# Splitting the 128-row transfers of a cross-entropy kernel into 32-row transfers

## The chip, the cores and the metric

The kernel runs on one core of a Trainium2 chip. The metric is the device time in microseconds of one execution; the times shown are medians of several executions.

## The reference

Two float32 matrices of 8192 x 8192 come in, and one goes out. Nothing is reduced: each output element depends on one element of each input.

```python
eps = 1e-7
pred = np.clip(pred, eps, 1 - eps)
return -(target * np.log(pred) + (1 - target) * np.log(1 - pred))
```

`target` holds zeros and ones only. The kernel uses that: for such a target the result is -log|target - 1 + pred|, so one logarithm is enough.

## The kernel before

The 67.1 million elements are taken as a flat list and cut into 37 chunks, numbered 0 to 36, from the end of the list to its beginning. A chunk is laid on all 128 partitions, so that partition p holds one contiguous piece of DRAM (`chunk`). Chunks 0 and 1 are 7680 columns wide, chunks 2 to 33 are 15360 wide (61440 bytes of float32 a row), chunks 34 and 35 are 7680 wide, and chunk 36 has 1696 columns. A further 45056 elements at the start of the list, "side", are held on 32 partitions and moved by SP in transfers of eight rows.

Two rings in on-chip memory hold the chunks: `ring_p`, float32, for `pred`, and `ring_t`, bfloat16, for `target`. The target is cast by the transfer itself. Each ring has two places of 15360 columns, which chunks take in turn, so chunk k + 2 goes where chunk k was. All arithmetic is done in place in `ring_p`, and the store reads from it. Therefore the load of pred of chunk k + 2 has to wait until the store of chunk k has read its last byte, whereas the load of its target needs only that DVE is done with the old one.

For each wide chunk the work is done in two halves of 7680 columns: DVE clips pred (L90) and adds target - 1 (L93), ACT takes the absolute value (L96) and the logarithm (L97), and DVE negates (L100). The order on each engine is written out by hand (`manual_schedule`). POOL issues almost all transfers, in this order for each chunk k: the store of chunk k (L76), the target load of chunk k + 2 (L71), the pred load of chunk k + 2 (L72). Its queue is in order: an instruction that waits holds those behind it. SP issues the first pred load, the side transfers and the last three stores. One transfer of 128 rows is spread over the core's 16 DMA engines, eight rows on each.

Chunk 33 is called z in the last part of the code, and chunks 34, 35 and 36 are a, b and c. The last loads are issued while chunk 32 is stored, and then the remaining stores drain.

Of the kernel before, what the change touches and what calls it, by code (L numbers as in the profile page):

```python
# [1 line left out]

# [4 lines left out]

EPS = 1e-7

BIG = 15 * 1024  # L10
HALF = BIG // 2
SIDE = 1408


def plan(total):

    n, last = divmod(total, BIG)
    assert n > 4 and 0 < last <= 2048
    spots = [(HALF, 0), (HALF, HALF)]
    spots += [(BIG, k % 2 * BIG) for k in range(1, n - 1)]  # L20
    end = (n - 1) % 2 * BIG
    return spots + [(HALF, end), (HALF, end + HALF), (last - SIDE // 4, 2 * BIG)]

@with_exitstack
def kernel(
    ctx: ExitStack,
    tc: tile.TileContext,
    pred: bass.AP,  # L30
    target: bass.AP,
    out: bass.AP,
):
    nc = tc.nc
    fp32 = mybir.dt.float32
    bf16 = mybir.dt.bfloat16
    Alu = mybir.AluOpType
    Act = mybir.ActivationFunctionType
    P = nc.NUM_PARTITIONS

    R, C = pred.shape
    spots = plan(R * C // P)
    n = len(spots)
    widths = [w for w, _ in spots]
    cols = [sum(widths[:k]) for k in range(n)]

    def chunk(ap, k):
        flat = ap.rearrange("r c -> (r c)")
        end = R * C - cols[k] * P
        return flat[end - widths[k] * P : end].rearrange("(p w) -> p w", p=P)  # L50

    pool = ctx.enter_context(tc.tile_pool(name="rings", bufs=1))
    ring = [P, 2 * BIG + widths[-1]]
    ring_p = pool.tile(ring, fp32, name="ring_p", tag="ring_p")
    ring_t = pool.tile(ring, bf16, name="ring_t", tag="ring_t")
    warm = pool.tile([1, 8], fp32, name="warm", tag="warm")
    side_p = pool.tile([32, SIDE], fp32, name="side_p", tag="side_p")
    side_t = pool.tile([32, SIDE], fp32, name="side_t", tag="side_t")

    def side(ap, j):  # L60
        flat = ap.rearrange("r c -> (r c)")
        return flat[: 32 * SIDE].rearrange("(p w) -> p w", p=32)[j:32:4]

    def spot(ring, k, part=(0, 1)):
        w, c = spots[k]
        i, m = part
        return ring[:, c + i * w // m : c + (i + 1) * w // m]

    def load(k):
        queue = nc.sync if k == 0 else nc.gpsimd  # L70
        nc.gpsimd.dma_start(out=spot(ring_t, k), in_=chunk(target, k))  # L71
        queue.dma_start(out=spot(ring_p, k), in_=chunk(pred, k))  # L72

    def store(k):
        queue = nc.sync if k >= n - 3 else nc.gpsimd
        queue.dma_start(out=chunk(out, k), in_=spot(ring_p, k))  # L76

    def load_side():
        nc.vector.memset(side_p[:, 0:2], 0.5)  # L79
        nc.vector.memset(side_t[:, 0:2], 0.0)  # L80
        for j in range(4):
            nc.sync.dma_start(out=side_t[j:32:4, :], in_=side(target, j))
            nc.sync.dma_start(out=side_p[j:32:4, :], in_=side(pred, j))

    def store_side():
        for j in range(4):
            nc.sync.dma_start(out=side(out, j), in_=side_p[j:32:4, :])

    def front_of(p, t):
        nc.vector.tensor_scalar(  # L90
            out=p, in0=p, scalar1=EPS, scalar2=1 - EPS, op0=Alu.max, op1=Alu.min
        )
        nc.vector.scalar_tensor_tensor(  # L93
            out=p, in0=t, scalar=1.0, in1=p, op0=Alu.subtract, op1=Alu.add
        )
        nc.scalar.activation(out=p, in_=p, func=Act.Abs)  # L96
        nc.scalar.activation(out=p, in_=p, func=Act.Ln)  # L97

    def back_of(p):
        nc.vector.tensor_scalar(out=p, in0=p, scalar1=-1.0, scalar2=None, op0=Alu.mult)  # L100

    def front(k, *part):
        front_of(spot(ring_p, k, *part), spot(ring_t, k, *part))

    def back(k, *part):
        back_of(spot(ring_p, k, *part))

    with tc.manual_schedule():
        nc.vector.memset(warm, 1.0)  # L109
        for k in range(3):  # L110
            load(k)
        nc.scalar.activation(out=warm, in_=warm, func=Act.Ln)  # L112
        front(0)
        front(1)
        back(0)
        store(0)
        back(1)
        store(1)
        load(3)
        for k in range(2, n - 4):  # L120
            front(k, (0, 2))
            front(k, (1, 2))
            back(k, (0, 2))
            back(k, (1, 2))
            store(k)
            if k == n - 6:
                load_side()
            if k == n - 5:
                front_of(side_p, side_t)
            for j in range(k + 2, n if k == n - 5 else k + 3):  # L130
                load(j)
        z, a, b, c = range(n - 4, n)
        front(z, (0, 2))
        back_of(side_p)
        store_side()
        front(z, (1, 2))
        back(z, (0, 2))
        front(a)
        back(z, (1, 2))
        store(z)  # L140
        front(b, (0, 2))
        front(b, (1, 2))
        back(a)
        store(a)
        front(c)
        back(b)
        store(b)
        back(c)
        store(c)


# [1 line left out]
_INS = ['pred', 'target']  # L153
_OUTS = [((8192, 8192), 'float32')]


# [23 lines left out]
```

## Time and profile before

| what | value |
|---|---|
| time, median of 3 executions | 1865.55 us (1865.36 to 1867.03) |
| profiled execution, span from its first to its last instruction | 1863.1 us |
| DVE, ACT, POOL busy in it | 1124.7, 902.1, 57.4 us |
| HBM read and written | 536.87 MB and 268.44 MB |
| transfers issued by POOL, by lines L71, L72, L76 | 37, 36, 34 |
| one POOL issue, mean | 0.53 to 0.54 us |

No time but its span is kept for the profiled execution; the median is 2.45 us above the span. The profile's page gives busy times of the engines, the share of time in which the 16 DMA engines moved packets, and the packets of each queue (q0 is POOL's, q1 is SP's). A packet here is one row of a transfer, or one small write that tells a semaphore of a completion. The trace holds a record of every packet with its size, start and duration, without the number of the DMA engine.

### The profile page before, as it was taken

Reading aid. Unit: us, or ns where it says so; the run is one execution under the profiler, and the core shown is the slowest. Engines: PE = TensorE matmul, PEld = TensorE weight load, DVE = VectorE, ACT = ScalarE, POOL = GpSimd, SP = SyncE. Lnnn points to the kernel's source line nnn. Section 1 sums busy time; section 2 is a strip of 40 time slices with the busy share of each in tenths; the row PEclk is TensorE's granted clock in tenths of the full one; section 3 lists DMA queues with packets and bytes.
Section 4 is the critical chain, followed back from the end, with each engine's and each line's share of the span. In section 5 each row is a group of like instructions: output and inputs, shape, how many; then the busy total and the mean of one; then the engine's idle time right before and its main releaser. Section 6 shows DMA issues by size and latency. Waiting matters only on the chain.

```text
span 1863.1 us, 649 instructions
## 1 busy us (share of the span) xinstructions
DVE 1124.7 (60%) x215; ACT 902.1 (48%) x144; POOL 57.4 (3%) x111
## 2 busy tenths in 40 slices
DVE  4655767555576655557665555766555576655585
ACT  3345553335555333555533355553335555333665
POOL 0000000000000000000000000000000000000000
DMA  9999999999999999999999999999999999999999
GB/s 295 378 356 343 352 344 367 383 385 348 348 352 344 370 384 383 347 352 351 346 370 385 383 347 352 351 346 370 385 383 346 352 352 346 370 384 379 352 340 392
DMA packets 16180, 671.22 MB, mean 360 GB/s; under 512 B 1872, under 2 KB 1872, under 8 KB 2352
## 3 DMA queue, kind: packets, MB, share of 16 engines
q0 software_dynamic: 15408, 657.98, 98.5%
q1 hardware_dynamic: 768, 13.21, 1.7%
q14 instruction: 4, 0.03, 0.0%
HBM read 536.87 MB, written 268.44 MB: 432 GB/s over the span
## 4 chain that ended last, share of the span: by engine, by line
DMA 35%; issue 26%; ACT 22%; DVE 15%; POOL 1%; DVEq 0%; POOLq 0%; PEldq 0%
DMA ring_p<-in_pred_dram 32%; ACT ring_p L96 11%; ACT ring_p L97 11%; DVE ring_p L93 7%; DVE ring_p L90 4%; DVE ring_p L100 4%; DMA out_dram<-ring_p 3%; POOL ring_t L71 0%; POOL out_dram L76 0%; DVEq L175 0%; POOL ring_p L72 0%; POOLq L76 0%; POOLq L71 0%; DVEq L90 0%; PEldq L175 0%
## 5 line engine op out<-in xcount | busy, mean ns | idle before, releaser
L96 ACT ACTIVATE ring_p<-ring_p 128x7680 f32<-128x7680 f32 (+1 forms) x70 | 450.3, 6433 | 932.2 <-DVE ring_p L93 932.2
L93 DVE SCALAR_TENSOR_TENSOR ring_p<-ring_t,ring_p 128x7680 f32<-128x7680 bf16 (+1 forms) x70 | 556.9, 7955 | 2.4
L90 DVE TENSOR_SCALAR ring_p<-ring_p 128x7680 f32<-128x7680 f32 (+1 forms) x70 | 283.8, 4055 | 396.7 <-DMA ring_p<-in_pred_dram 396.7
L100 DVE TENSOR_SCALAR ring_p<-ring_p 128x7680 f32<-128x7680 f32 (+1 forms) x69 | 283.8, 4115 | 321.2 <-ACT ring_p L97 321.2
L97 ACT ACTIVATE ring_p<-ring_p 128x7680 f32<-128x7680 f32 (+1 forms) x70 | 450.8, 6440 | 2.2
L72 POOL DMA_DIRECT2D ring_p<-in_pred_dram x36 | 19.2, 532 | 909.3 <-DMA out_dram<-ring_p 909.3
L76 POOL DMA_DIRECT2D out_dram<-ring_p x34 | 18.4, 541 | 851.3 <-DVE ring_p L100 827.0
L71 POOL DMA_DIRECT2D ring_t<-in_target_dram x37 | 20.0, 542 | 0.8 <-PEq L175 0.8
L96 ACT ACTIVATE side_p<-side_p 32x1408 f32<-32x1408 f32 x1 | 1.4, 1375 | 6.7 <-DVE side_p L93 6.7
L112 ACT ACT_TABLE_LOAD x1 | 1.3, 1283 | 0.7 <-PEq L164 0.7
L93 DVE SCALAR_TENSOR_TENSOR side_p<-side_t,side_p 32x1408 f32<-32x1408 f32 x1 | 1.6, 1611 | 0.0
L97 ACT ACTIVATE side_p<-side_p 32x1408 f32<-32x1408 f32 x1 | 1.4, 1375 | 0.0
L90 DVE TENSOR_SCALAR side_p<-side_p 32x1408 f32<-32x1408 f32 x1 | 0.9, 874 | 0.0
L100 DVE TENSOR_SCALAR side_p<-side_p 32x1408 f32<-32x1408 f32 x1 | 0.9, 874 | 0.0
L109 DVE MEMSET warm<- 1x8 f32 x1 | 0.1, 65 | 0.8 <-PEq L164 0.8
L112 ACT ACTIVATE warm<-warm 1x8 f32<-1x8 f32 x1 | 0.2, 209 | 0.0
L164 POOL MEMSET const-float32-0.0<- 128x1 f32 x1 | 0.1, 99 | 0.2 <-issue 0.2
L164 POOL MEMSET const-bfloat16-1.0<- 128x1 bf16 x1 | 0.1, 102 | 0.0
L164 POOL MEMSET const-float32-1.0<- 128x1 f32 x1 | 0.1, 99 | 0.0
L164 POOL MEMSET const-uint8-127<- 128x1 uint8 x1 | 0.1, 99 | 0.0
L79 DVE MEMSET side_p<- 32x2 f32 x1 | 0.1, 60 | 0.0
L80 DVE MEMSET side_t<- 32x2 f32 x1 | 0.1, 60 | 0.0
## 6 DMA issues: line engine op xcount, KB each, us to landing
ring_p<-in_pred_dram POOLq DMA_DIRECT2D x32, 7680.0 KB, 35.9
out_dram<-ring_p POOLq DMA_DIRECT2D x32, 7680.0 KB, 29.2
ring_t<-in_target_dram POOLq DMA_DIRECT2D x32, 3840.0 KB, 46.8
ring_p<-in_pred_dram POOLq DMA_DIRECT2D x3, 3840.0 KB, 35.6
ring_t<-in_target_dram POOLq DMA_DIRECT2D x4, 1920.0 KB, 27.9
out_dram<-ring_p POOLq DMA_DIRECT2D x2, 3840.0 KB, 27.1
out_dram<-ring_p SPq DMA_DIRECT2D x2, 3840.0 KB
ring_p<-in_pred_dram SPq DMA_DIRECT2D x1, 3840.0 KB
```

The costliest lines, as they stand in the source:

```text
L71: nc.gpsimd.dma_start(out=spot(ring_t, k), in_=chunk(target, k))
L72: queue.dma_start(out=spot(ring_p, k), in_=chunk(pred, k))
L76: queue.dma_start(out=chunk(out, k), in_=spot(ring_p, k))
L79: nc.vector.memset(side_p[:, 0:2], 0.5)
L80: nc.vector.memset(side_t[:, 0:2], 0.0)
L90: nc.vector.tensor_scalar(out=p, in0=p, scalar1=EPS, scalar2=1 - EPS, op0=Alu.max, op1=Alu.min)
L93: nc.vector.scalar_tensor_tensor(out=p, in0=t, scalar=1.0, in1=p, op0=Alu.subtract, op1=Alu.add)
L96: nc.scalar.activation(out=p, in_=p, func=Act.Abs)
L97: nc.scalar.activation(out=p, in_=p, func=Act.Ln)
L100: nc.vector.tensor_scalar(out=p, in0=p, scalar1=-1.0, scalar2=None, op0=Alu.mult)
L112: nc.scalar.activation(out=warm, in_=warm, func=Act.Ln)
L164: nc = _bacc.Bacc("TRN2", target_bir_lowering=False, num_devices=1)
```

## The change

For chunks 1 to 33 every transfer of 128 rows becomes four of 32 rows: group g covers partitions 32g to 32g + 31. The DRAM side is viewed as eight by four rows, so that a transfer can be spread over eight DMA engines with four rows each; within a group the rows come to partitions in another order than before, the same for pred, target and output. Groups are taken in the order 0, 2, 1, 3, that is lower and upper 64 partitions in turn. For k = 2 to 31 `store_and_load` mixes the store of chunk k with the target load of chunk k + 2: on the lower partitions the two store groups come before the two target groups, on the upper partitions target group 2 comes ahead of store groups 2 and 3, and target group 3 behind them. The pred loads follow. Loads and stores of chunks 0, 34, 35 and 36 stay whole. The arithmetic is unchanged.

```diff
+    def group(ap, k, g):
+        rows = chunk(ap, k)[32 * g : 32 * g + 32]
+        return rows.rearrange("(b a) w -> a b w", b=4)
+
+    def load_group(k, g, ring, src):
+        nc.gpsimd.dma_start(out=spot(ring, k)[32 * g : 32 * g + 32], in_=group(src, k, g))
+
+    def store_group(k, g):
+        nc.gpsimd.dma_start(out=group(out, k, g), in_=spot(ring_p, k)[32 * g : 32 * g + 32])
+
+    def grouped(k):
+        return 0 < k < n - 3
+
     def load(k):
+        if grouped(k):
+            for ring, src in ((ring_t, target), (ring_p, pred)):
+                for g in (0, 2, 1, 3):
+                    load_group(k, g, ring, src)
+            return
         queue = nc.sync if k == 0 else nc.gpsimd
...
     def store(k):
+        if grouped(k):
+            for g in (0, 2, 1, 3):
+                store_group(k, g)
+            return
...
+    def store_and_load(k, j):
+        if not (grouped(k) and grouped(j)):
+            store(k)
+            load(j)
+            return
+        store_group(k, 0)
+        load_group(j, 2, ring_t, target)
+        store_group(k, 1)
+        store_group(k, 2)
+        load_group(j, 0, ring_t, target)
+        store_group(k, 3)
+        load_group(j, 1, ring_t, target)
+        load_group(j, 3, ring_t, target)
+        for g in (0, 2, 1, 3):
+            load_group(j, g, ring_p, pred)
...
-            store(k)
+            store_and_load(k, k + 2)
             if k == n - 6:
                 load_side()
             if k == n - 5:
                 front_of(side_p, side_t)
-            for j in range(k + 2, n if k == n - 5 else k + 3):
-                load(j)
+                for j in range(k + 3, n):
+                    load(j)
```

## The prediction

> **What bounds the kernel now.** I read the page first: which engine is full. Section 1, then the DMA rows of sections 2 and 3:
>
> ```profile
> DVE 1124.7 (60%) x215; ACT 902.1 (48%) x144; POOL 57.4 (3%) x111
> ...
> DMA  9999999999999999999999999999999999999999
> ...
> DMA packets 16180, 671.22 MB, mean 360 GB/s; under 512 B 1872, under 2 KB 1872, under 8 KB 2352
> ...
> q0 software_dynamic: 15408, 657.98, 98.5%
> q1 hardware_dynamic: 768, 13.21, 1.7%
> ...
> HBM read 536.87 MB, written 268.44 MB: 432 GB/s over the span
> ```
>
> No compute engine passes 60%; the 16 DMA engines are full in all 40 slices. MB counts what lands, so a target cast to bf16 counts half, and the HBM line is the load that matters. The packet counts decode: POOL's 107 transfers give 107 x (128 rows + 16 small packets) = 15408, and those 107 x 16 = 1712 small ones, with SP's 160, are the 1872 under 512 B. They are the completion writes, one for each engine of a transfer. On q1, SP's 4 wide transfers give 4 x 144 and its 12 side transfers of 8 rows 12 x (8 + 8), together 768: eight rows went over eight engines.
>
> Next the busy time by stretches (steady state, then the drain; the last two numbers are DMA share and GB/s), and the waits:
>
> ```profile
> 1109.00:1218.00 109.00, 65.73 (x12) 52.60 (x8) 3.19 (x6) 1.00 1.00 361
> ...
> 1822.00:1863.00 41.00, 22.45 (x8) 21.86 (x7) 0.00 (x0) 1.00 0.93 397
> ```
>
> ```profile
> POOL ring_p L72 <- DMA out_dram<-ring_p: 909.3, 32, 29.2
> POOL out_dram L76 <- DVE ring_p L100: 827.0, 33, 52.5
> DVE ring_p L90 <- DMA ring_p<-in_pred_dram: 396.7, 36, 18.5
> ```
>
> POOL's long waits look like the bound and are not: while it waits, the rings still hold work. The timeline of one chunk shows the reserve:
>
> ```profile
> 1166.98 4.16 DVE L90 TENSOR_SCALAR ring_p<-ring_p 128x7680 f32<-128x7680 f32 x1 [11.37 <-DMA ring_p<-in_pred_dram]
> ...
> 1185.39 0.53 POOL L72 DMA_DIRECT2D ring_p<-in_pred_dram  x1 [28.42 <-DMA out_dram<-ring_p]
> ...
> 1210.22 0.54 POOL L76 DMA_DIRECT2D out_dram<-ring_p  x1 [24.30 <-DVE ring_p L100]
> 1210.75 0.54 POOL L71 DMA_DIRECT2D ring_t<-in_target_dram  x1
> ...
> 1221.33 4.16 DVE L90 TENSOR_SCALAR ring_p<-ring_p 128x7680 f32<-128x7680 f32 x1 [11.40 <-DMA ring_p<-in_pred_dram]
> ```
>
> L90 starts when a chunk lands: 1221.33 - 1166.98 = 54.35 us per chunk. The store enters the queue at 1210.22, 11.1 us before the pred load ahead of it has landed, so the rings never run dry.
>
> **What is left to gain.** The trace's packet records give size, start and duration. A row of 61440 bytes takes 2267 ns, and the next starts 2263.5 ns after it: 27.14 GB/s per engine, for plain and cast rows alike. All the data, 805.3 MB / 16 / 27.14 GB/s = 1854.3 us. Add 2.0 us before the first packet and 1.0 from the last packet (1862.1) to the end of the span: 1857.3. Against 1863.1 that leaves 5.8 us, 0.31%, for any reordering of the same rows. Part of it is stalls: 89 rows took over 2285 ns, in sum 28.2 us over 16 engines, a mean of 1.76 us. Nearly all are the eighth, last row of a pred load, just before the engine turns from loads to the store: 0.60 us a mean engine at 73 us, 0.19 at 128, 0.17 at 183, almost none after 680 us, when the engines have drifted apart. Four engines have 2.2 to 3.7 us of stalls and lag the other twelve by 3 us at 1600 us; the twelve lost 1.4 on average. Eight engines carry the side rows besides (12 packets of some 221 ns, 2.7 us), so the last packets of all engines fall between 1859.1 and 1862.1.
>
> **The change, part by part.**
>
> *Bytes and rows.* Rows stay 61440 bytes; the permutation inside 32 rows is the same for pred, target and output. Four rows on each of eight engines for each transfer, and the alternation, keep eight full rows per engine and tensor: 24 x 2263.5 ns = 54.32 us per chunk as now. Zero, if the halves go to different engines.
>
> *Transfers.* Chunks 1 to 33 are grouped: 33 x 12 = 396 transfers in place of 99, 297 more. On POOL each issue takes 0.54 us, 160 us more in all, 12 x 0.54 = 6.5 us per 54.35; POOL is 3% busy. The last of four stores is issued five issues, 2.7 us, after the first, under the 11.1 us of queue. Hidden; with that cover gone, 2.7 us per chunk, 89 us.
>
> *Waits.* The instruction listing of the built program shows eight completion semaphores in turn, so a transfer also waits for the eighth before it. Take the issue of store group 0 as zero. Pred groups 1 and 3 of the chunk before end at 11.1, and only then may target groups 1 and 3 go out; by then each half has three transfers of 4 x 2.2635 = 9.05 us queued, to 38.3. POOL sits in that wait, and the pred loads behind it: group 0 needs store 0 (20.2), groups 1 and 2 stores that end at 29.2, group 3 store 3 at 38.3; their own turns come at 47.3 and 56.4. So the shortest cover in POOL's queue is 18.1 us. Moving target 2 ahead makes the upper store one slot later and its completion too, already counted here. L90 now waits for four pieces, but the last lands when the whole did. Zero.
>
> *Completions.* If each grouped transfer writes one on all 16 engines, as POOL's 107 did, each engine has 297 more. The records have 9 ns for most and 22 after a cast, mean 13.5; between rows they push the next row by 6 to 8. At 9 ns: 297 x 9 = 2.7 us, on the path, since the engines are full. Bounds: 6 ns gives 1.8, 13.5 gives 4.0; eight writers as on SP's side rows leave 99 more per engine, 0.9; below nothing is excluded, since a packet cannot take negative time. [...]
>
> *Casts.* The first plain row behind a cast takes 2280 in place of 2267 ns. The upper half now turns from targets to others twice per chunk: 33 x 13 ns = 0.4 us on eight engines, 0 on the others. I count 0, taking the side rows' engines for the ones that end last and for the lower half's; the 0.4 stays in the range.
>
> *Stalls.* Now the halves turn to stores 9 us apart, eight engines at a time. No row shows this. Bounds: nothing comes back (0), or all does: the twelve's 1.4 us, or 2.0 if the last engine (1862.1) falls to the 1860.1 that most would reach. I take 1.4: the stalls belong to the moments when all 16 turn within a microsecond, and four engines that turned 3 us after twelve no longer stalled.
>
> *Start and end.* At the start, chunks 1 and 2 issue in small pieces behind 18 us of chunk 0. In the drain the last grouped store is issued within 1.6 us where it took 0.54, just as the loads end (1818.4 against 1821): at most 1 us on the later half, beside last packets that already spread over 3 us. Zero.
>
> **Sum:** 1863.1 + 2.7 - 1.4 = 1864.4 in the span. The median is 2.45 above the span (1865.55 - 1863.1), kept: 1866.9, 0.07% slower.
>
> **Rivals.**
>
> 1. *Stalls return every chunk: slower.* One half now reads HBM while the other writes for 18 us in every chunk, and regrouping might hold eight engines in step. For it: engines in step stalled by 0.19 us per chunk at 128 us. Against: twelve writing beside four reading late in the run show none. Price 33 x 0.19 = 6.3, less the 1.76 there now, plus 2.7: 1872.8. It decides from 0.08 us per chunk: 33 x 0.08 + 2.7 - 1.76 = 3.6 us. At 0.60 each, 1886.
>
> 2. *Completions are dear:* 4.0 us, nothing back, 0.4 on the path: 1870.0.
>
> 3. *Completions hide, all stalls go: faster.* 1865.55 - 2.0 = 1863.6. If the lagging engines alone set the end, up to 3.7 less: 1861.9; the least is the floor above, 1857.3 + 2.45 = 1859.8. Against: most engines end within 1.5 us of the last, side rows or not, so one cause hardly moves all of them.
>
> 4. *The halves do not overlap: much slower.* If a transfer of 32 rows kept the other eight engines idle, 396 x 9.05 us, less 4 half rows for chunk 1's 12 (54 us), are 3530 us in place of half: some 1765 more, 3630. Rows of before cannot refute it, since they hold no two half-wide transfers in one queue that fill it. Against: rows of the timeline show that transfers queue ahead, and an engine starts its next row 3 to 8 ns after a completion's start, without waiting for other engines. [...]
>
> 5. *The change does not do what it says:* two rows on each of 16 engines. The completions come the same, the stalls stay: 1868.3.
>
> **How the numbers follow.** What a measurement of this kernel can tell from no change is about 0.2%, 3.7 us: 1861.8 to 1869.3. Forecast 0.47 (own range 1864.5, with eight writers and half the stalls back, to 1868.3, with none back): same. Rival 1: 0.22, slower. Rival 2: 0.08, slower. Rival 3: 0.14, of which 0.10 between the floor and 1861.8 and 0.04 same. Rival 4: 0.04, slower. Rival 5: 0.05, same. Faster 0.10, same 0.56, slower 0.34. The range runs from 1863.2 (rival 3 at its first price inside, its quicker end out) to 1874, rival 1 at its first price with a microsecond above; outside lie rival 4, the dear end of rival 1 and the quick end of rival 3, together some 0.2.
>
> **What would show it.** In the page after: q0 with 396 x 48 + 8 x 144 = 20160 packets and 6624 under 512 B (16992 and 3456 with eight writers). L90 starts 54.4 us apart from the first chunks on, where they are now 54.9 apart (76.59 to 131.49). POOL near 404 x 0.54 = 218 us, with no wait that leaves a DMA slice under 9. Rows over 2285 ns rare. Wrong: chunks above 54.5 us apart throughout (rival 1), half the GB/s (rival 4), or chunks at 54.35 and a span under 1861 (rival 3).

## The result, and the profile after

The changed kernel takes 1876.45 us (median of 4, 1872.62 to 1877.15) against 1865.94 for the kernel before: ratio 1.0053, 95% interval 1.0041 to 1.0066. That is 10.5 us slower, outside the range on record (1863.2 to 1874.0). The profiled execution has a span of 1874.1 us, 11.0 more than before. Ratios leave out executions over 1.5% above the fastest of their kernel, of which only the kernel with sixteen engines, below, had any: two of six.

The page of the changed kernel, the rows of busy time and of packets:

```profile
DVE 1124.7 (60%) x215; ACT 902.1 (48%) x144; POOL 391.9 (21%) x408
...
DMA  9999999999999999999999999999999999999999
...
DMA packets 33609, 671.33 MB, mean 358 GB/s; under 512 B 19296, under 2 KB 19296, under 8 KB 19776
...
q0 software_dynamic: 32832, 658.05, 98.7%
q1 hardware_dynamic: 768, 13.21, 1.7%
...
HBM read 536.87 MB, written 268.44 MB: 430 GB/s over the span
```

The DMA engines are full in every slice, as before, and move the same bytes. The halves work side by side: between 1000 and 1700 us, eight cast rows (a target's) and eight plain rows are under way together for 26% of the time, in the kernel before for 0.1%. The packets under 512 B are the news: 19296 where the forecast had 6624. Of them 160 are SP's, so POOL's queue holds 19136. Its 8 whole transfers account for 8 x 16 = 128; the other 19008 are 48 for each of the 396 grouped transfers, not 16. The trace's semaphore records tell them apart. POOL's eight completion semaphores rise 6464 times, which is 404 x 16, exactly 16 for each transfer; before they rose 107 x 16 = 1712 times. So the completions came as forecast, and two in three of a piece's small packets, 32 of 48, raise none of these semaphores.

The waits, the timeline of one late chunk, and two stretches (steady state and drain, with DMA share and GB/s last):

```profile
POOL ring_p L74 <- DMA out_dram<-ring_p: 636.3, 88, 11.2
POOL out_dram L77 <- DVE ring_p L138: 454.3, 32, 32.0
DVE ring_p L128 <- DMA ring_p<-in_pred_dram: 407.6, 36, 18.5
...
POOL ring_t L74 <- DMA ring_p<-in_pred_dram: 234.4, 58, 8.3
```

```profile
1163.47 0.55 POOL L77 DMA_DIRECT2D out_dram<-ring_p  x1 [13.31 <-DVE ring_p L138]
...
1172.91 0.55 POOL L74 DMA_DIRECT2D ring_t<-in_target_dram  x1 [6.21 <-DMA ring_p<-in_pred_dram]
1174.74 4.16 DVE L128 TENSOR_SCALAR ring_p<-ring_p 128x7680 f32<-128x7680 f32 x1 [11.56 <-DMA ring_p<-in_pred_dram]
1174.94 4.07 POOL L74 DMA_DIRECT2D ring_t<-in_target_dram  x1 [1.48 <-DMA ring_p<-in_pred_dram]
...
1229.33 4.16 DVE L128 TENSOR_SCALAR ring_p<-ring_p 128x7680 f32<-128x7680 f32 x1 [11.64 <-DMA ring_p<-in_pred_dram]
```

```profile
1109.00:1218.00 109.00, 65.73 (x12) 52.61 (x8) 23.82 (x25) 1.00 1.01 361
1833.00:1874.00 41.00, 22.37 (x8) 21.86 (x7) 0.54 (x1) 1.00 0.91 390
```

The wait of the target loads on the pred loads (the shared completion semaphores) has come as forecast, 234.4 us of it, and the store still enters the queue 11.3 us before the next landing. So no wait sets the pace; but the chunk late in the run takes 54.59 us (1229.33 - 1174.74) where it took 54.35. Over the late chunks the mean is 54.56 against 54.35: 0.2 us for each chunk, which brings 33 more small packets for a mean engine than before. Chunks early in the run are slower still; these landings are 55.1 and 55.2 apart, where the same chunks were 54.8 and 54.5 apart before:

```profile
131.63 4.16 DVE L128 TENSOR_SCALAR ring_p<-ring_p 128x7680 f32<-128x7680 f32 x1 [12.05 <-DMA ring_p<-in_pred_dram]
186.77 4.16 DVE L128 TENSOR_SCALAR ring_p<-ring_p 128x7680 f32<-128x7680 f32 x1 [12.18 <-DMA ring_p<-in_pred_dram]
241.95 4.16 DVE L128 TENSOR_SCALAR ring_p<-ring_p 128x7680 f32<-128x7680 f32 x1 [12.24 <-DMA ring_p<-in_pred_dram]
```

The packet records give a sum. Between the first and the last packet, the time of one mean engine is the time of its rows, plus that of its small packets less what packets overlap, plus idle time (fewer than 16 packets under way). The sum closes by definition, since the small packets' column is what rows and idle time leave over; that it is a price of small packets is for the experiments to show. In us per engine:

| kernel | first to last packet | rows | stalls within the rows | small packets less overlap | idle |
|---|---|---|---|---|---|
| before | 1860.07 | 1865.25 | 1.8 | -6.91 | 1.73 |
| changed | 1871.05 | 1868.53 | 5.5 | +0.41 | 2.11 |
| difference | 10.98 | 3.28 | 3.7 | 7.33 | 0.38 |

A stall is counted where a plain row (pred or output, 61440 bytes) takes over 2285 ns, or a cast row (a target's) over 2295, as the excess over 2267 or 2281. So two thirds of the loss stand in the small packets' column: 17424 more of them, 1089 per engine, 7.33 us, 6.7 ns each. One third is rows that stall; 2.9 of the changed kernel's 5.5 us are cast rows, where the kernel before had 0.04. The experiments test both.

### The profile page after: what moved, and what is told of

The parts are those of the page before. It is cut to its first block, busy times and chain, and to the rows that moved or that the text cites. A ratio compares the mean times of both kernels' runs of the same rounds, so it can differ in the third digit from the quotient of the medians.

```text
span 1874.1 us, 1112 instructions
## 1 busy us (share of the span) xinstructions
DVE 1124.7 (60%) x215; ACT 902.1 (48%) x144; POOL 391.9 (21%) x408
## 2 busy tenths in 40 slices
DMA packets 33609, 671.33 MB, mean 358 GB/s; under 512 B 19296, under 2 KB 19296, under 8 KB 19776
## 4 chain that ended last, share of the span: by engine, by line
DMA 50%; ACT 24%; DVE 15%; issue 8%; POOL 3%; DVEq 0%; POOLq 0%; PEldq 0%
DMA ring_p<-in_pred_dram 26%; DMA out_dram<-ring_p 24%; ACT ring_p L134 12%; ACT ring_p L135 12%; DVE ring_p L131 7%; DVE ring_p L128 4%; DVE ring_p L138 4%; POOL ring_p L74 1%; POOL out_dram L77 1%; POOL ring_t L74 1%; DVEq L213 0%; POOL ring_t L89 0%; DVEq L128 0%; POOLq L77 0%; POOLq L90 0%
## 5 line engine op out<-in xcount | busy, mean ns | idle before, releaser
L131 DVE SCALAR_TENSOR_TENSOR ring_p<-ring_t,ring_p 128x7680 f32<-128x7680 bf16 (+1 forms) x70 | 556.8, 7955 | 2.4
L128 DVE TENSOR_SCALAR ring_p<-ring_p 128x7680 f32<-128x7680 f32 (+1 forms) x70 | 283.8, 4055 | 407.6 <-DMA ring_p<-in_pred_dram 407.6
L138 DVE TENSOR_SCALAR ring_p<-ring_p 128x7680 f32<-128x7680 f32 (+1 forms) x69 | 283.8, 4114 | 321.3 <-ACT ring_p L135 321.3
L74 POOL DMA_DIRECT2D ring_p<-in_pred_dram x132 | 130.7, 994 | 676.4 <-DMA out_dram<-ring_p 636.3
L74 POOL DMA_DIRECT2D ring_t<-in_target_dram x132 | 184.5, 1400 | 248.7 <-DMA ring_p<-in_pred_dram 234.4
L77 POOL DMA_DIRECT2D out_dram<-ring_p x132 | 74.2, 568 | 475.1 <-DVE ring_p L138 454.3
L90 POOL DMA_DIRECT2D ring_p<-in_pred_dram x3 | 1.7, 559 | 27.7 <-DMA out_dram<-ring_p 27.7
L98 POOL DMA_DIRECT2D out_dram<-ring_p x1 | 0.6, 573 | 11.9 <-DVE ring_p L138 11.9
L89 POOL DMA_DIRECT2D ring_t<-in_target_dram x4 | 2.4, 600 | 1.5 <-PEq L213 0.8
L131 DVE SCALAR_TENSOR_TENSOR side_p<-side_t,side_p 32x1408 f32<-32x1408 f32 x1 | 1.6, 1614 | 0.0
L138 DVE TENSOR_SCALAR side_p<-side_p 32x1408 f32<-32x1408 f32 x1 | 0.9, 876 | 0.0
L128 DVE TENSOR_SCALAR side_p<-side_p 32x1408 f32<-32x1408 f32 x1 | 0.9, 875 | 0.0
```

Of the source, the lines that this page charges most:

```text
L74: nc.gpsimd.dma_start(out=spot(ring, k)[32 * g : 32 * g + 32], in_=group(src, k, g))
L77: nc.gpsimd.dma_start(out=group(out, k, g), in_=spot(ring_p, k)[32 * g : 32 * g + 32])
L128: nc.vector.tensor_scalar(out=p, in0=p, scalar1=EPS, scalar2=1 - EPS, op0=Alu.max, op1=Alu.min)
L131: nc.vector.scalar_tensor_tensor(out=p, in0=t, scalar=1.0, in1=p, op0=Alu.subtract, op1=Alu.add)
```

## The experiments

Each ratio is against the kernel before on the same chip. Theory A says the small packets cost what the table says; theory S says that stalls belong to the first part of the run, where engines turn from loads to stores nearly in step.

### Sixteen engines for 32 rows

```diff
     def group(ap, k, g):
-        rows = chunk(ap, k)[32 * g : 32 * g + 32]
-        return rows.rearrange("(b a) w -> a b w", b=4)
+        return chunk(ap, k)[32 * g : 32 * g + 32]
```

> The changed kernel with the 32 rows of a transfer left in their order (no eight-by-four view), so that it can go over sixteen engines with two rows each; same groups, same order of transfers. Theory A (completions): the changed kernel's 7 us of steady loss (chunks 54.55 us apart against 54.35) come from 48 small writes per grouped transfer, three on every engine; with sixteen engines there is one each, 396 x 16 + 128 = 6464 on POOL's queue, and chunks late in the run are 54.35 + 0.21 x 9/33 = 54.41 us apart; time 1867 to 1870. Rival B: the three writes come with any 32-row transfer of POOL; 19136 small packets again and 54.55. Rival C (ports): sixteen engines in 32 partitions get in each other's way, so that chunks are far over 55 us apart, towards twice the time.

Measured: 2570.40 us (median of four, 2557.59 to 2586.60), ratio 1.378 (1.374 to 1.383).

```profile
DMA packets 20937, 671.28 MB, mean 263 GB/s; under 512 B 6624, under 2 KB 6624, under 8 KB 7104
...
HBM read 536.87 MB, written 268.44 MB: 315 GB/s over the span
```

Two things follow. The small packets are 6624, as A said: 16 for each grouped transfer, so the 48 belong to transfers on eight engines, and B falls. And the time is where C put it, in the rows: 640 of the 693 us that a mean engine takes longer. Plain rows have a median of 3330 ns, and a quarter take over 4544, about twice 2267; cast rows keep a median of 2281. Why plain rows slow down and cast rows do not, no run shows, nor does a trace show the ports of C's name. With the eight-by-four view, in the changed kernel, the same pieces took 1876.45 us.

### Which pieces cost what

Only the targets in pieces (pred and out whole). In the three kernels of this section, and in the two under "The law of the small packets", the rows of one tensor alone come in the order of the pieces, so they meet other rows of pred or target or come out in another order; the bytes and the transfers are what is compared.

```diff
-            for ring, src in ((ring_t, target), (ring_p, pred)):
-                for g in (0, 2, 1, 3):
-                    load_group(k, g, ring, src)
+            for g in (0, 2, 1, 3):
+                load_group(k, g, ring_t, target)
+            nc.gpsimd.dma_start(out=spot(ring_p, k), in_=chunk(pred, k))
             return
...
     def store(k):
-        if grouped(k):
-            for g in (0, 2, 1, 3):
-                store_group(k, g)
-            return
...
-        if not (grouped(k) and grouped(j)):
+        if True:
```

> Only the targets go in 32-row transfers over eight engines; pred loads and stores are whole as in the kernel before, in the order of before. Theory A: per chunk and engine 12 + 2 small writes, against 3 before and 36 in the changed kernel: late chunks 54.35 + 0.21 x 11/33 = 54.42 us apart, +2.3 us over the run; stalls as before: 1868.3 us. Rival: the loss belongs to stores or pred loads in pieces, and this is at 1866; or to cast pieces, and this is at 1872 or more.

Measured: 1867.74 us, ratio 1.0010 (1.0002 to 1.0019); late chunks 54.42 us apart.

```profile
DMA packets 21989, 671.25 MB, mean 360 GB/s; under 512 B 7680, under 2 KB 7680, under 8 KB 8160
```

7680 less SP's 160 is 7520: 132 x 48 + 74 x 16. The small packets' term rose by 2.78 us, 7.7 ns for each of 363 per engine, and the stalls are 1.3. Stores alone in pieces, and then pred loads alone, the latter also with the last edit of the former (the stores of a chunk all ahead of the next target, as before):

```diff
     def load(k):
-        if grouped(k):
-            for ring, src in ((ring_t, target), (ring_p, pred)):
-                for g in (0, 2, 1, 3):
-                    load_group(k, g, ring, src)
-            return
...
-        if not (grouped(k) and grouped(j)):
+        if True:
```

```diff
-            for ring, src in ((ring_t, target), (ring_p, pred)):
-                for g in (0, 2, 1, 3):
-                    load_group(k, g, ring, src)
+            nc.gpsimd.dma_start(out=spot(ring_t, k), in_=chunk(target, k))
+            for g in (0, 2, 1, 3):
+                load_group(k, g, ring_p, pred)
             return
...
     def store(k):
-        if grouped(k):
-            for g in (0, 2, 1, 3):
-                store_group(k, g)
-            return
```

> Only the stores of chunks 1 to 33 go in 32-row transfers over eight engines (rows of the output come permuted within groups); loads whole, order as before. Theory A: 7520 small packets, 363 more per engine, at 6.7 to 7.7 ns each +2.4 to 2.8 us, late chunks 54.42 us apart, as with the targets alone. Theory S: the pieces of the stores are what adds the changed kernel's 3.8 us of stalls, since each half now turns by itself: stalls 3 to 5 us, time 1870 to 1872. Rival: stalls stay at 1.2 to 1.8, time 1868.

> Only the pred loads of chunks 1 to 33 go in 32-row transfers over eight engines (pred rows meet other rows of target); targets and stores whole, order as before. Theory A: 7520 small packets, +2.4 to 2.8 us, late chunks 54.42 us apart. If the pieces of the pred loads are what adds the stalls: stalls 3 to 5 us and 1870 to 1872 us; if not, 1.2 to 1.8 us and 1868.

Measured: stores 1869.07 us, ratio 1.0020 (1.0011 to 1.0029), small packets +2.20 us, stalls 2.6; pred loads 1867.43 us, ratio 1.0012 (1.0004 to 1.0021), small packets +2.34, stalls 1.2. Theory A holds three times, at 6.1 to 7.7 ns a packet. The three small-packet terms add to 7.3 us, the changed kernel's own 7.33. The stalls do not add: +0.8 (stores), -0.6 (pred loads) and -0.5 (targets). The 3 to 5 us that S expected of the stores did not come. These three kernels also lack the mixed order, so what they are to be compared with is all three tensors in pieces without it, two sections on: +3.6. No one tensor in pieces makes them.

### When the pieces come

```diff
     def grouped(k):
-        return 0 < k < n - 3
+        return 17 <= k < n - 3
```

The complement has `0 < k < 17` in that line.

> The changed kernel with chunks 1 to 16 whole as before, and 17 to 33 in pieces with the mixed order. Theory A: 204 grouped transfers, 10688 small packets, 561 more per engine, +3.8 us; chunks after 1000 us 54.55 apart. Theory S (stalls belong to the first part of the run): stalls stay near 1.8, so 1869.5 us. Rival (stalls belong to the first dozen chunks after the pieces begin): 2 to 3.8 us more of them after 950 us, 1872 to 1873.

> The changed kernel with chunks 1 to 16 in pieces and in the mixed order, and 17 to 33 whole: the complement of the late grouping. Theory A: 192 grouped transfers, 10160 small packets, 528 more per engine, +3.5 us. Theory S (stalls belong to the first part of the run, and pieces make them more): 5.5 us of stalls per engine, 3.7 more than before: 1865.4 + 3.5 + 3.7 = 1872.6 us. Rival (the added stalls came of something else than pieces early in the run): 1869.

Late grouping: 1869.07 us, ratio 1.0020 (1.0012 to 1.0029).

```profile
DMA packets 25158, 671.27 MB, mean 360 GB/s; under 512 B 10848, under 2 KB 10848, under 8 KB 11328
```

```profile
1005.29 4.16 DVE L128 TENSOR_SCALAR ring_p<-ring_p 128x7680 f32<-128x7680 f32 x1 [11.64 <-DMA ring_p<-in_pred_dram]
1059.81 4.16 DVE L128 TENSOR_SCALAR ring_p<-ring_p 128x7680 f32<-128x7680 f32 x1 [11.57 <-DMA ring_p<-in_pred_dram]
1114.39 4.16 DVE L128 TENSOR_SCALAR ring_p<-ring_p 128x7680 f32<-128x7680 f32 x1 [11.63 <-DMA ring_p<-in_pred_dram]
```

This is the cleanest price of the small packets, since nothing else moved: stalls 2.0 (+0.2), all rows -0.14, idle +0.02, small packets +3.76 us for 561 per engine, 6.7 ns each. The median moved by 3.8. Chunks are 54.52 and 54.58 apart as soon as the pieces begin.

The complement measured 1873.83 us (1871.37 to 1877.03), ratio 1.0039 (1.0025 to 1.0053). Its profiled execution was its slowest, with 8.3 us of stalls and small packets +3.61. With the mixed order, then, the added stalls are there only when pieces begin early, as S said; without it that does not hold, as the next section shows. Times differ from one execution of the complement to the next by up to 5.7 us, so one profiled execution does not fix the amount. POOL's long issues (see below) are not what makes the stalls by themselves: the late grouping has 32 of them and 2.0 us of stalls against 1.8 before.

### The mixed order

```diff
     def store_and_load(k, j):
-        if not (grouped(k) and grouped(j)):
+        if True:
             store(k)
             load(j)
             return
```

First on the changed kernel, then on the late grouping:

> The changed kernel with the stores of chunk k all ahead of the targets of chunk k+2 in the order 0, 2, 1, 3, without the upper half's target ahead of its store. As many transfers and completions. Theory A: late chunks 54.55 us apart as in the changed kernel. Theory S (stalls at turns between loads and stores): the turn of the upper half 9 us after the lower's costs the cast rows 2.9 us per engine in the first half of the run; with both halves turning at once these go, the pred rows' stalls are as before (1.8) or as now (2.6): 1872 to 1874 us. Rival: the mixed order spares something, and without it the stalls of pred rows grow: 1878 or more.

> The late grouping (chunks 17 to 33 in pieces) without the mixed order: stores of a chunk ahead of the targets, 0, 2, 1, 3. Small packets as with the late grouping, 10688, +3.8 us. If the mixed order is worth something by itself (the 5 us between the changed kernel and the one without the mix), about half of it is lost here: 1871 to 1872 us, with chunks after 1000 us over 54.6 us apart, and engines ending further apart. Rival: the mix matters only while engines are in step, early; then 1869 us, as the late grouping.

Measured: 1881.42 us, ratio 1.0081 (1.0068 to 1.0094), against the changed kernel's 1.0053 (1.0041 to 1.0066); and 1873.60, ratio 1.0035 (1.0021 to 1.0049), against the late grouping's 1869.07, which ran on another chip. My expectation for the first, fewer stalls, was a miss, and its rival came: cast rows stall less without the mix (0.6 us against 2.9), but plain rows stall more (4.8 against 2.6). The "early alone" rival for the second was a miss too. On the full change, loading the upper half's target ahead of its store spares some 5 us, clear of the noise. On the late grouping it is 4 us when each kernel is taken against the kernel before on its own chip, and the two intervals overlap; there it shows in the rows: stalls are 5.4 us without the mix and 2.0 with it, at the same 10688 small packets, though 0.9 of that difference lies before 900 us, where the two kernels still do the same. On the full change stalls were 5.4 without and 5.5 with the mix, but not in the same part of the run: with the mix 0.2 us come after 950 us, without it 3.2 do. There idle time made the difference, 6.7 us per engine against 2.1, most of it in the drain, which stretches out:

```profile
1822.00:1881.00 59.00, 37.33 (x12) 29.73 (x8) 4.10 (x4) 1.00 0.87 360
```

### Time, addresses and the start

Chunks from the beginning of the list instead of its end:

```diff
-        end = R * C - cols[k] * P
-        return flat[end - widths[k] * P : end].rearrange("(p w) -> p w", p=P)
+        start = 32 * SIDE + cols[k] * P
+        return flat[start : start + widths[k] * P].rearrange("(p w) -> p w", p=P)
```

> The kernel before, with the chunks taken from the beginning of the list to its end (the same transfers, the other order of addresses). Theory S (stalls belong to the first part of the run, while engines turn nearly in step): stalls of about 1.8 us per engine again before 700 us, little after, time within 1 us of before. Rival (stalls belong to addresses): they come in the second half of the run, after 1200 us, or in another amount altogether.

Measured: 1865.28 us, ratio 1.0002 (0.9993 to 1.0011); stalls 1.9 us, again nearly all before 800 us. In the kernel before they belong to the first part of the run, not to places in memory.

The side loads at the start, on the kernel before:

```diff
         for k in range(3):
             load(k)
+        load_side()
...
-            if k == n - 6:
-                load_side()
```

> The kernel before, with the eight side transfers moved from near the end to the start of SP's queue (the same bytes; eight of the engines get 1.8 us of extra rows at the start, not at the end). Theory S (stalls come when engines in step turn together, and fade as they drift): engines are apart from the first chunk on, the 1.76 us of stalls fall to under 1, and the time falls by 0.5 to 1.5 us, to about 1865. Rival: stalls depend on addresses or on the time in the run, not on step: stalls stay at 1.8, time within 0.5 us of the kernel before.

Measured: 1869.87 us, ratio 1.0020 (1.0011 to 1.0029); stalls 5.0 us. A miss, in sign too: the side rows at the start, meant to set eight engines behind, came with more stalls, not fewer. Extra rows on eight engines are therefore not enough to end them; how far the engines were apart was not measured.

### The law of the small packets

Both kernels start from the one with the targets alone in pieces. The first has pieces of 16 rows over eight engines, in the order 0, 4, 1, 5, 2, 6, 3, 7 (its `load_group` takes 16 partitions accordingly); the second has pieces of 32 rows over four engines:

```diff
-        rows = chunk(ap, k)[32 * g : 32 * g + 32]
-        return rows.rearrange("(b a) w -> a b w", b=4)
+        rows = chunk(ap, k)[16 * g : 16 * g + 16]
+        return rows.rearrange("(b a) w -> a b w", b=2)
```

```diff
-        return rows.rearrange("(b a) w -> a b w", b=4)
+        return rows.rearrange("(b a) w -> a b w", b=8)
```

> As the kernel with the targets alone in pieces, but in pieces of 16 rows over eight engines, two rows each (targets meet other rows of pred): 264 pieces. Theory A1 (48 small packets per transfer whatever its rows): 264 x 48 + 74 x 16 = 13856, 759 more per engine than before, at 7 to 7.7 ns +5.3 to 5.8 us: 1871. Rival A2 (16, and one per row): 264 x 32 + 1184 = 9632, +3.3 to 3.8 us: 1869.

> As the kernel with the targets alone in pieces, with the rows of a piece viewed as four by eight, so that it goes over four engines with eight rows each (targets meet other rows of pred): 132 pieces. If the small packets grow as the engines of a transfer fall, there are more than 48 for each (80 would make 11744 in all); if eight is no special number and they depend on the rows, 48 again and 7520, time 1868 as with eight engines.

Measured: 1885.51 us, ratio 1.0107 (1.0093 to 1.0120), and 1897.01 us, ratio 1.0167 (1.0153 to 1.0181). The packet rows, sixteen rows first:

```profile
DMA packets 24103, 671.28 MB, mean 356 GB/s; under 512 B 9792, under 2 KB 9792, under 8 KB 10272
```

```profile
DMA packets 30437, 671.28 MB, mean 354 GB/s; under 512 B 16128, under 2 KB 16128, under 8 KB 16608
```

Less SP's 160 and 74 x 16 of whole transfers, that is 8448 / 264 = 32 and 14784 / 132 = 112 per piece. With 48 (32 rows, eight engines) and 16 (32 rows, or 128, on sixteen) one rule fits all five: 16 + rows x (16 / engines - 1), with the engines that each view is laid out for. Rows and small packets together are then 16 x (rows / engines + 1) for each transfer, 48, 80 and 144 for the three kinds of pieces on fewer than sixteen engines. This is a fit to the counts; how the packets are shared among the engines is not shown, since the records have no engine's number. In both kernels, too, POOL's semaphores rise 16 times for each transfer. The times miss both expectations: the small packets' terms are only 4.3 and 4.5 us, 8.7 and 5.1 ns a packet; the rest, 16.3 and 27.5 us, is in rows that stall throughout the run. A price for each added transfer instead of each packet would fit worse: it would be 25 ns of an engine in the changed kernel, 19 and 46 here. Why these smaller or narrower pieces stall so much was not tried.

## Why the prediction was wrong, point by point

- **What bounds the kernel:** right. The DMA engines stayed full in all 40 slices, and the added packets went into the time, 7.33 of the 10.98 us.
- **Bytes, rows, halves:** right. Rows kept 2267 and 2281 ns late in the run. Rival 4 is refuted: a chunk takes 54.6 us, not about twice that, HBM moves 430 GB/s, and eight cast and eight plain rows are under way together for 26% of the time.
- **Transfers and waits:** right in effect, wrong in size. POOL is busy 391.9 us, not 218, because some issues took up to 4.3 us beside DVE's L128 and L138 (4.07 at 1174.94 above, ending with L128): 66 issues took over 0.7 us, and 65 of them overlap one of the two. The DMA engines never ran out of work for it: they are full in all 40 slices, so the 18.1 us of cover, an estimate, was enough.
- **Completions:** this is the step that failed. The term was 297 x 9 ns = 2.7 us. The price per packet was near (6.7 ns, inside the bounds of 6 and 13.5), and the completions came as counted, 16 for each transfer: 6464 rises for 404. That a grouped transfer has 16 as well no run of before showed. But the number of small packets was not that of the completions: 1089 more per engine, 7.3 us, because each piece on eight engines brings 32 others. POOL's rows of before held only transfers on all 16 engines, where every small packet is a completion, and I took one per engine from them as the upper bound for a kind of transfer that they did not contain. With 7.3 in its place and no stall recovered, the sum would have been 1872.9, still inside the range; it took the stalls as well to leave it.
- **Stalls:** the second failure, in sign. I took 1.4 us back; in the profiled executions 3.7 more came. Rival 1 had the direction, at 6.3 us as a price for every chunk; in fact they fade by about 950 us. Its sign, chunks above 54.5 us apart throughout, came all the same, but late in the run it came of the small packets: that sign could not tell the two apart. The argument that eight engines turning by themselves would stall less was an inference from one kernel's late rows; the changed kernel itself, with 5.5 us of stalls against 1.8, speaks against it, and so does moving the side loads, with 5.0.
- **The forecast's own range:** its lower end of 1864.5 is not what it names. Eight writers (0.9) and half the stalls back (0.7 to 1.0) give 1865.4 to 1865.8; 1864.5 takes the full 2.0.
- **Casts, start and end:** too small to tell apart; idle time rose by 0.4 us.

What is not settled is why rows stall, and why all three tensors in pieces make more of it while one alone does not. In the kernel before, stalls come early in the run and do not follow addresses. In the changed kernel 5.4 of 5.5 us come before 950 us; the cast rows among them end 6 to 12 us after a landing, when by the order of issue the lower half stores and the upper half loads targets, and most of the plain rows end in the last 5 us before a landing, where the pred loads do. Without the mixed order, stalls go on after 950 us, 3.2 of 5.4 us on the full change and 2.4 of 5.4 on the late grouping, so theory S does not cover them. No variant beat the kernel before.

## What to carry to other kernels

Before splitting a transfer on a full DMA queue, count the packets that each piece brings for a mean engine, those that carry no rows included, and price them in full (here 5.1 to 8.7 ns each); a trace that has no such transfer gives no upper bound, so a small probe belongs ahead of the estimate. A count of small packets is not yet a count of completions: the rises of the semaphores tell the two apart. When pieces of 32 partitions are needed all the same, spread each over eight engines, as the eight-by-four view does, rather than over sixteen (1876.45 us here against 2570.40); here it also helped to interleave loads and stores between the halves (1876.45 us against 1881.42). A stall whose cause is not known should be put into a sum with both signs, because a change of the transfers can move it either way: here by -0.6 us with the pred loads alone in pieces, by +3.2 with the side loads moved.

## What the runs showed of the hardware that I had not expected

A POOL transfer spread over fewer than 16 engines brought more small packets the more rows it had: 32 for 16 rows and 48 for 32 rows on eight engines, 112 for 32 rows on four, each some 5 to 9 ns of an engine. Only 16 for each transfer raised a completion semaphore, in each of these shapes. Sixteen engines in the same 32 partitions brought plain rows from 2267 ns to a median of 3330, a quarter of them over 4544, and left cast rows at a median of 2281. POOL's issues of transfers took up to 4.3 us in place of 0.54 beside DVE's float32 clip and negation (L128, L138), and not beside L131, which reads bfloat16 as well: 118 issues beside it alone took 0.53 to 0.57 us.
